# A whole masked last tile, the samples' state as the moving operand, and a head's squares in one row

## The chip, the cores and the metric

One core of one Trainium2 chip runs the whole program. The metric is the device time of one execution in microseconds, the median of the runs taken.

## What is computed

The reference is one inference step of a trunk of two layers with D = 1024. The input is a prompt of 2064 tokens (16 learned ones and 2048 more) and a group of 8 samples with one token each and a state from before. Each layer is `x <- LayerNorm(alpha*x + mixer(x))`. The mixer projects x to 10 x 512 channels and 8 gates, runs three groups of heads on them and projects the result back:

- A, a gated linear recurrence over time;
- B, retention: 4 heads of 128 channels; a score of key by query times a fixed decay, and a state S of 128 x 128 that decays and gains key by value;
- C, the gated delta rule: 4 heads of 128 channels; keys are normed, each token has a decay and a strength, and a chunk of 64 tokens needs the inverse of a triangular matrix of its keys' products; it too carries a state S of 128 x 128 per head.

```python
v_new = u - jnp.einsum('bhik,bhkv->bhiv', w, s)
att = jnp.einsum('bhid,bhjd->bhij', q, k) * decay
o = jnp.einsum('bhik,bhkv->bhiv', q * jnp.exp(gc)[..., None], s) + jnp.einsum('bhij,bhjv->bhiv', att, v_new)
s = s * jnp.exp(g_last)[..., None] + jnp.einsum('bhik,bhiv->bhkv', k * jnp.exp(g_last - gc)[..., None], v_new)
```

The samples take one such step each, from their own state, and everything is in float32. The outputs are the new activations and all new states.

## The kernel before

Each layer goes over its tokens in two halves (`sblock`): 1024 prompt tokens, then 1040 prompt tokens and the 8 samples. A half is a row of stages (`STAGES`): four K stages (the delta heads' keys), and then the heads of the groups A, B and C, one stage each. A stage projects its channels: 24 matmuls for each slab of 128 channels and each block of 512, 384 or 280 tokens (x and the weights are split in a high and a low float32r part, three products). Into these the head work of earlier stages is mixed: it is written as generators, and a `Pump` takes a step of them after so many projection matmuls. After both halves come the output projection with the LayerNorm, row tile by row tile, and into it the samples' work is mixed in the same way (`samples_delta`, `samples_ret`).

That order is not the final one. A `Recorder` notes every operation with a cost, simulates the engines and writes each engine's instructions in the order in which they came out (`order`): of the operations that are ready, the earliest noted goes first. All instructions are issued by this, so nearly all have line 273 in the profile, and they are told apart by their tiles. The order on each engine is then fixed. TensorE's, VectorE's, ScalarE's, GpSimd's and SP's queues each run in that order; hardware semaphores hold back what isn't ready.

The names that the change touches:

- `tl` in `sblock` lists a half's groups: two of 4 tiles with 128 tokens, and in the second half one more tile of 16 tokens, the tail. Its third entry, `R`, is the tile's height, and all work on the tail is cut to `R`: tiles of 16 rows, 16 columns, or both.
- `gates_c` makes the gates of all tokens as columns (`gtok`, `gg`, `bt`), `valid` masks the empty rows of the ninth tile.
- `keys_bg` makes for each delta head the decay matrix (`pdt`: two float32r matmuls and a bfloat16 one) and the squares of its keys in chunks of 64 (`pk`: 128 rows, 64 columns of weights, 64 moving columns; two chunks side by side in the array's column halves). There is one PSUM tile `pk` for a group of 4 tiles, and a generator step behind each.
- `inverses` and `solve` invert the triangular matrices; the tail's has 16 rows.
- `delta_bg` runs a delta head: `prep` (transposes `ptk`, `ptv`, `ptq`, products with the inverse `pw` and `pu`, keys by queries `qk`), `chain` (from chunk to chunk: the state's product `pz`, its update `pd`), `outs` (`po`), `norm` (`pno`). For the tail, `chain` reads the state with two products, `pz<-stg,wt` and `pz<-stg,qT`.
- `retention_bg` runs a retention head with tiles of 128 tokens: `prep` (`qk`, `ptk`, `ptv`), `chain` (scores by values, the state's product, its update `pd`), and at the end a norm and `pno`. For the tail the products are `po<-tk`, `po<-str,qT` and `pd<-tk`.
- `samples_delta` and `samples_ret` load a head's 8 states of 128 x 128 (`sv`) and multiply each as weights with two columns (key and query) or one (query): `ps<-swork,sv` and `ps<-scol,sv`. Then `outer` forms the new states.

In float32 a matmul of the program is two MATMUL instructions in the profile, each with a weight load of its own; a transpose is one.

```python
for b in range(NS):
    PE.matmul(pb[:, 16 + 2 * b:18 + 2 * b], sv[:, 0, b], kq[:, h, b], start=True, stop=True)
```

Of the kernel before, what the change touches and what calls it, by code (L numbers as in the profile page):

```python
# [343 lines left out]
def hymba_step(ctx: ExitStack, tc: tile.TileContext, x0t, x0, win, wab, wout, wg, vec, fbc, const, rope,  # L344
# [31 lines left out]
    mean_l = C("ones128").to_broadcast([128, 128])  # L376
    identb = cst.tile([128, 128], BF, name="identb")
# [25 lines left out]
    def pz2():  # L403
        return [psum.tile([128, 512], F32, tag="pz", name="pz", bufs=2).rearrange("p (t c) -> p t c", t=4)
                for _ in range(2)]
# [150 lines left out]
    def layer(l):  # L556
# [43 lines left out]
        def sblock(sb):  # L600
# [71 lines left out]
            tl = [(0, 4, 128), (4, 4, 128)] + ([(8, 1, 16)] if samp else [])  # L672
# [34 lines left out]
            def gates_c():  # L707
# [3 lines left out]
                if samp:  # L711
                    G.memset(gtok[:, 8], 0.0)
                for t in range(NT):
                    n = min(128, ts - t * 128)
                    PE.transpose(pg[:n, t, :], gab[:16, t * 128:t * 128 + n], ident[:16, :16])
                for n, ta, tb in ((128, 0, 8), (24, 8, 9))[:1 + samp]:
                    V.tensor_copy(gtok[:n, ta:tb], pg[:n, ta:tb, 0:8])
                    V.tensor_tensor(gtok[:n, ta:tb], gtok[:n, ta:tb], pg[:n, ta:tb, 8:16], op=OP.add)
# [6 lines left out]
                if samp:  # L725
                    V.tensor_tensor(gg, gg, C("valid").unsqueeze(2).to_broadcast([128, 9, 4]), op=OP.mult)
# [3 lines left out]
                V.tensor_scalar(bt[:, :NT], bt[:, :NT], 0.5, 0.5, op0=OP.mult, op1=OP.add)  # L730

# [12 lines left out]
                if samp:  # L744
                    G.memset(ssk[:, 8], 0.0)
# [21 lines left out]
            def keys_bg(h, kT):  # L767
                dt = wk.tile([128, 9, 64], F32, tag="dt", name="dt", bufs=1)
                for t4, nt, R in tl:
                    m = min(64, R)  # L770
                    gm, gl = (wk.tile([128, 4, 64], F32R, tag="gm", name="gm", bufs=2) for _ in range(2))
                    for e, x in enumerate((gm, gl)):
                        V.tensor_tensor(x[:R, :nt, :m], C("maskc")[:R, :m].unsqueeze(1).to_broadcast([R, nt, m]),
                                        ggp[:R, e, t4:t4 + nt, h:h + 1].bitcast(F32).to_broadcast([R, nt, m]),
                                        op=OP.mult)
                    pd = pt("pdt")[:, :256].rearrange("p (t i) -> p t i", i=64)
                    for e, x in enumerate((gm, gl)):
                        PE.matmul(pd[:R, :nt, :m], m1r[:R, :R], x[:R, :nt, :m], start=(e == 0), stop=False)
                    PE.matmul(pd[:R, :nt, :m], identb[:R, :R],
                              negb[:R, :m].unsqueeze(1).to_broadcast([R, nt, m]), start=False, stop=True)  # L780
                    A.activation(dt[:R, t4:t4 + nt, :m], pd[:R, :nt, :m], AF.Exp)
# [921 lines left out]
    for l in range(DEPTH):  # L1703
        layer(l)
# [107 lines left out]
```

## Time and profile before

| | us |
|---|---|
| median of 3 runs | 3141.41 |
| lowest, highest | 3139.7, 3144.42 |
| the profiled execution | 3134.19 |
| its span, first to last instruction | 3132.2 |

The span holds 47396 instructions. In the profile an engine's busy time is the union of its instructions; matmuls are pipelined, and their ends are modelled, so the time from one matmul's start to the next tells more than its duration. PE is the matmul part of TensorE and PEld its weight loads, DVE is VectorE, ACT ScalarE, POOL GpSimd. The view in order of time merges neighbouring instructions of one form into a row: start, latency from the first start to the last end, engine, line, operation, output and inputs, shape of the array (rows*columns), the moving operand, and the count. Some matmul records can be missing from a trace, so a count may be low by one.

### The profile page before, as it was taken

The page shows a single profiled execution, that of the slowest core. Times are in us where ns is not written, and L with a number is a line of the kernel's source. Part 1 is how long each engine was busy: PE and PEld are TensorE (multiplying, and loading weights), DVE is VectorE, ACT ScalarE, POOL GpSimd, SP SyncE. Part 2 cuts the span into 40 slices and gives each one's busy share as a digit, 9 for nine tenths or more (in the row PEclk, how much of TensorE's full clock was granted, in tenths as well). Part 3 has the DMA queues.
Part 4 walks back from the last instruction along what each step waited for, and adds up shares of the span by engine and source line. Part 5 has one row for each costly group of instructions (what it writes and reads, how often), then busy time and mean ns, then how long its engine had stood idle before and what let it go on. Part 6 is the DMA issues. An engine that isn't in the chain of part 4 may idle for free. (4 is left out here: it accounts for less than half of the span.)

```text
span 3132.2 us, 47396 instructions
## 1 busy us (share of the span) xinstructions
PE 3089.2 (99%) x18876; PEld 2707.9 (86%) x18876; DVE 2038.0 (65%) x3736; ACT 1294.2 (41%) x2732; POOL 678.5 (22%) x651
## 2 busy tenths in 40 slices
PE   8999999999999999999999999999999999999999
PEld 6888888899999999788778888888999999997886
DVE  6976565679756565656469765655897565656564
ACT  4455444543454454311144544444434544543100
POOL 2222132222222231011022222222222222311110
PEclk9999999999999999999999999999999999999999
DMA  4121111321111113555231212112211111136641
GB/s 154 63 70 48 57 50 58 110 82 51 49 54 59 46 57 96 179 175 168 95 115 56 70 48 66 52 57 96 85 50 50 54 59 43 61 92 195 183 145 59
DMA packets 137060, 262.96 MB, mean 84 GB/s; under 512 B 24368, under 2 KB 79600, under 8 KB 136840
## 3 DMA queue, kind: packets, MB, share of 16 engines
q1 hardware_dynamic: 113640, 179.91, 18.5%
q0 software_dynamic: 23200, 80.04, 7.1%
q8 instruction: 148, 2.42, 0.3%
q14 instruction: 72, 0.59, 0.1%
HBM read 195.13 MB, written 65.04 MB: 83 GB/s over the span
## 5 line engine op out<-in xcount | busy, mean ns | idle before, releaser
L273 PE MATMUL pj<-arena 128*128 128x512 f32 (+3 forms) x9760 | 2114.1, 360 | 14.3 <-ACT arena L273 7.6
L273 PEld LDWEIGHTS pj<-arena 128*128 128x128 f32 (+1 forms) x9760 | 1625.5, 187 | 170.6 <-ACT arena L273 8.2
L273 POOL TENSOR_TENSOR arena<-raw,arena 128x1024 fp32r<-128x1024 f32 x159 | 399.5, 2512 | 1077.5 <-ACT arena L273 886.4
L273 ACT CAST arena<-raw 128x1024 fp32r<-128x1024 f32 x180 | 189.0, 1050 | 302.4 <-PE pj L273 163.9
L273 DVE SCALAR_TENSOR_TENSOR stg<-stg,eg,pd 128x128 f32<-128x128 f32 x264 | 90.8, 344 | 117.6 <-PE pd L273 116.4
L273 PE MATMUL pj<-arena,ah 128*128 128x512 f32 x512 | 166.0, 401 | 1.3 <-ACT arena L273 1.3
L273 ACT COPY ur<-pj 128x512 f32<-128x512 f32 (+2 forms) x160 | 80.4, 503 | 146.1 <-PE pj L273 146.0
L273 ACT ACT_TABLE_LOAD x106 | 136.0, 1283 | 4.5 <-DVE vT L273 1.9
L273 ACT COPY sw<-pj 64x512 f32<-64x512 f32 (+2 forms) x160 | 79.9, 500 | 103.2 <-PE pj L273 65.7
L273 PEld LDWEIGHTS pj<-arena,ah 128*128 128x128 f32 x512 | 96.7, 189 | 24.5 <-ACT arena L273 1.8
L273 PE MATMUL pj<-arena,al 128*128 128x512 f32 (+1 forms) x296 | 111.6, 398 | 0.1
L273 ACT ACTIVATE g<-pj 128x512 f32<-128x512 f32 (+2 forms) x120 | 61.8, 515 | 109.9 <-PE pj L273 108.9
L273 PE MATMUL pd<-kv 128*128 128x128 f32 x512 | 99.9, 277 | 3.5 <-DVE kv L273 2.6
L273 PEld LDWEIGHTS pz<-stg,wq 128*128 128x128 f32 x512 | 89.7, 189 | 12.5 <-DVE stg L273 2.7
L273 PE MATMUL pz<-stg,wq 128*128 128x128 f32 x512 | 99.6, 276 | 0.8 <-DVE stg L273 0.4
L273 PEld LDWEIGHTS pd<-kv 128*128 128x128 f32 x512 | 86.8, 190 | 13.7 <-issue 2.8
L273 DVE SCALAR_TENSOR_TENSOR g<-g,pj 128x512 f32<-128x512 f32 (+2 forms) x120 | 69.5, 579 | 39.5 <-ACT g L273 38.5
L273 ACT ACTIVATE wq<-pz,eg 64x128 f32<-64x128 f32 x128 | 44.1, 361 | 122.9 <-DVE kv L273 55.1
L273 PE MATMUL po<-arena,ah 128*128 128x512 f32 x288 | 93.9, 400 | 0.0
L273 ACT CAST bh<-mb 128x512 fp32r<-128x512 f32 x32 | 19.6, 620 | 171.3 <-PE po L273 107.9
L273 DVE SCALAR_TENSOR_TENSOR qT<-ur,gcw,qT 128x1024 f32<-128x1024 f32 (+1 forms) x48 | 75.0, 1562 | 18.4 <-ACT qT L273 18.3
L273 DVE SCALAR_TENSOR_TENSOR kT<-ur,gcw,kT 128x1024 f32<-128x1024 f32 (+1 forms) x48 | 74.0, 1541 | 19.2 <-ACT kT L273 18.7
(388 smaller groups left out, 5057.7 us busy)
## 6 DMA issues: line engine op xcount, KB each, us to landing
raw<-in_win SPq DMA_DIRECT2D x160, 512.0 KB, 3.3
ma<-mix_d SPq DMA_DIRECT2D x31, 512.0 KB, 5.1
mix_d<-g POOLq DMA_DIRECT2D x24, 520.0 KB, 3.3
mix_d<-g POOLq DMA_DIRECT2D x24, 512.0 KB, 3.4
raw<-in_wout SPq DMA_DIRECT2D x24, 512.0 KB, 4.4
xr<-in_x SPq DMA_DIRECT2D x16, 512.0 KB, 5.1
x_d<-yo POOLq DMA_DIRECT2D x16, 512.0 KB, 3.3
sv<-row_d POOLq DMA_DIRECT2D x16, 512.0 KB, 4.7
```

Of the source, the lines that this page charges most:

```text
L273: return lambda *args, **kw: self._r.note(self._n, op, lambda: f(*args, **kw), args, kw)
```

## The change

- The tail becomes a whole tile: the last 128 tokens of the prompt's second half (columns `np_ - 128` to `np_`), of which only the last 16 count. Masks and zeros (`cl`, loaded once by four small DMAs after two clears) keep the other 112 out: gates and strengths are multiplied by `tmask`, retention's key and score decays come from `tkdec` and `tdec`, and the delta head's inverse lies in the last 16 columns of a cleared tile. All tail matmuls have 128 rows and 128 columns then; the two reads of the state in the delta head's chain become one. The delta tail borrows group 0's `wq` and attention tile and the tile `ttbd` of the inverses. Its decay matrix is made in 128 x 64, and one DMA stores or loads all of a head's decay matrices where there were two.
- The squares of a head's keys are written one behind the other, without a step between, all 16 into one PSUM bank; the tail's two squares go to a second bank.
- The samples' products take the state as the moving operand (`from_state`): eight products with 32 columns of weights, of which one or two count, in the array's four column strips, 128 moving columns each; ScalarE copies the 128 x 256 result, and two transposes bring it back to columns.

The diff, cut to its core (elsewhere it replaces `:R` by whole tiles in the same way):

```diff
--- before.py
+++ after.py
...
+    cl = cst.tile([128, 13], F32, name="cl")
+    tmask, tkdec, tdec, teps = cl[:, 0:1], cl[:, 1:5], cl[:, 5:9], cl[:, 9:13]
+    def tail_constants():
+        G.memset(cl[:, 0:9], 0.0)
+        G.memset(teps, EPS)
+        a = _C["dret"][0] + 127
+        for dst, src in ((tmask, const[0:16, _C["ones"][0]:_C["ones"][1]]),
+                         (tkdec, const[0:16, _C["kdect"][0]:_C["kdect"][1]]),
+                         (tdec, const[0:16, a:a + 385:128]),
+                         (teps, const[0:16, _C["epsr"][0]:_C["epsr"][1]])):
+            SP.dma_start(dst[112:128], src)
...
-            tl = [(0, 4, 128), (4, 4, 128)] + ([(8, 1, 16)] if samp else [])
...
+                    c0 = min(t * 128, np_ - 128)
+                    PE.transpose(pg[:, t, :], gab[:16, c0:c0 + 128], ident[:16, :16])
...
+                    V.tensor_tensor(gg[:, 8], gg[:, 8], tmask.to_broadcast([128, 4]), op=OP.mult)
...
+                    V.tensor_tensor(bt[:, 8], bt[:, 8], tmask.to_broadcast([128, 4]), op=OP.mult)
...
-                for t4, nt, R in tl:
-                    m = min(64, R)
-                    pk = pt("pk")[:, :256].rearrange("p (t i) -> p t i", i=64)
+                pks = [pt("pk").rearrange("p (t i) -> p t i", i=64) for _ in range(1 + samp)]
+                pks = [pks[0][:, 0:4], pks[0][:, 4:8], pks[-1][:, 0:1]]
+                for (t4, nt, c0), pk in zip(tl, pks):
                     for i in range(nt):
-                        for o in range(0, R, 64):
-                            c0 = (t4 + i) * 128 + o
-                            PE.matmul(pk[o:o + m, i, :m], kT[:, c0:c0 + m], kT[:, c0:c0 + m],
-                                      start=True, stop=True)
-                    if R == 128:
+                        for o in (0, 64):
+                            cc = slice(c0 + i * 128 + o, c0 + i * 128 + o + 64)
+                            PE.matmul(pk[o:o + 64, i], kT[:, cc], kT[:, cc], start=True, stop=True)
+                for (t4, nt, c0), pk in zip(tl, pks):
+                    if nt == 4:
                         V.tensor_tensor(ap[:, t4:t4 + 4, h, :], pk, dt[:, t4:t4 + 4], op=OP.mult)
                     else:
-                        V.tensor_tensor(apt[:16, :, h], pk[:16, 0, :16], dt[:16, 8, :16], op=OP.mult)
+                        V.tensor_tensor(apt[:, :, h], pk[96:128, 0, 48:64], dt[96:128, 8, 48:64], op=OP.mult)
                     gm = wk.tile([128, 4, 64], F32, tag="gm", name="gm", bufs=2)
-                    V.tensor_tensor(gm[:R, :nt, :m], pk[:R, :nt, :m],
-                                    C("id64")[:R, :m].unsqueeze(1).to_broadcast([R, nt, m]), op=OP.mult)
-                    V.tensor_reduce(out=ssk[:R, t4:t4 + nt, h], in_=gm[:R, :nt, :m], axis=AX, op=OP.add)
-                    yield
-                G.dma_start(dt_d[h, :, :512], dt[:, :8].rearrange("p t i -> p (t i)"))
-                if samp:
-                    G.dma_start(dt_d[h, :16, 512:528], dt[:16, 8, :16])
+                    V.tensor_tensor(gm[:, :nt], pk, C("id64").unsqueeze(1).to_broadcast([128, nt, 64]), op=OP.mult)
+                    V.tensor_reduce(out=ssk[:, t4:t4 + nt, h], in_=gm[:, :nt], axis=AX, op=OP.add)
+                    yield
+                G.dma_start(dt_d[h, :, :64 * NT], dt[:, :NT].rearrange("p t i -> p (t i)"))
...
-                        q.wt, q.at = small("wt", [128, 16]), small("at", [16, 16])
+                        q.wq, q.at, q.cis = gs[0].wq, gs[0].at, (1,)
...
+                    else:
+                        A.copy(ttbd[96:128, 0, 112:128], apt[:, :, h])
+                        G.memset(ttbd[96:128, 0, 96:112], 0.0)
+                        G.tensor_copy(q.wq[:, 0, 2], qT[:, c0 + 64:c0 + 128])
...
-                        A.copy(q.wt, pw[:, 0, :R])
+                        A.copy(q.wq[:, 0, 3], pw[:, 0, 64:128])
+                        G.tensor_copy(kk[64:128, 0], kk[64:128, 1])
+                        G.memset(kk[0:64, 0], 0.0)
...
-                        for ci, (o, n) in enumerate(((0, 64), (64, 64)) if q.R == 128 else ((0, 16),)):
+                        for ci in q.cis:
                             pz = q.pz[i // 2][:, i % 2, ci]
-                            if q.R == 128:
-                                PE.matmul(pz, q.wq[:, i, 2 * ci:2 * ci + 2].rearrange("p e c -> p (e c)"), S,
-                                          start=True, stop=True)
-                            else:
-                                PE.matmul(pz[:16], q.wt, S, start=True, stop=True)
-                                PE.matmul(q.pz[0][:16, 0, 1], qT[:, q.c0:q.c0 + 16], S, start=True, stop=True)
-                            if q.R == 128:
-                                V.tensor_tensor(uv[o:, 1, i], uv[o:, 0, i], pz[o:], op=OP.add)
-                            else:
-                                V.tensor_tensor(uv[:n, 1, i], uv[:n, 0, i], pz[:n], op=OP.add)
+                            PE.matmul(pz, q.wq[:, i, 2 * ci:2 * ci + 2].rearrange("p e c -> p (e c)"), S,
+                                      start=True, stop=True)
+                            o = 64 * ci if nt == 4 else 0
+                            V.tensor_tensor(uv[o:, 1, i], uv[o:, 0, i], pz[o:], op=OP.add)
                             yield
                             ps = p1("pd")
-                            if q.R == 128:
-                                PE.matmul(ps[:, :128], kk[:, 1 - ci, i], uv[:, 1, i], start=True, stop=True)
-                            else:
-                                PE.matmul(ps[:, :128], kk[:n, 1, i], uv[:n, 1, i], start=True, stop=True)
+                            PE.matmul(ps[:, :128], kk[:, 1 - ci, i], uv[:, 1, i], start=True, stop=True)
...
+            def from_state(pb, sv, cols, c0, n):
+                pr = pt("psv").rearrange("p (s c) -> p s c", s=4)
+                for b in range(NS):
+                    j = 32 * (b % 4)
+                    PE.matmul(pr[j:j + 32, b // 4], cols[:, c0 + n * b:c0 + n * b + 32], sv[:, 0, b], start=True, stop=True)
+                rw = wk.tile([128, 2, 128], F32, tag="gm", name="rw", bufs=2)
+                A.copy(rw, pr[:, 0:2])
+                for s in range(2):
+                    PE.transpose(pb[:, 128 + 128 * s:256 + 128 * s], rw[:, s], ident)
+                return pb[:, 128:384].rearrange("p (b e) -> p b e", e=32)
...
-                    for b in range(NS):
-                        PE.matmul(pb[:, 16 + 2 * b:18 + 2 * b], sv[:, 0, b], kq[:, h, b], start=True, stop=True)
-                    pv = pb[:, 16:32].rearrange("p (b e) -> p b e", e=2)
+                    pv = from_state(pb, sv, swork, 16 * h, 2)
...
-                    for b in range(NS):
-                        PE.matmul(pb[:, b:b + 1], sv[:, 0, b], qs[:, h, b:b + 1], start=True, stop=True)
-                    V.scalar_tensor_tensor(out=o[:, h], in0=pb[:, 0:8], scalar=GAM[h], in1=o[:, h],
+                    pv = from_state(pb, sv, scol.rearrange("p c e h b -> p (c e h b)"), 128 + 8 * h, 1)
+                    V.scalar_tensor_tensor(out=o[:, h], in0=pv[:, :, 0], scalar=GAM[h], in1=o[:, h],
...
+                    if q.last:
+                        V.scalar_tensor_tensor(out=sn[:, 0, 0], in0=pa[:, 0], scalar=tdec[:, h:h + 1],
+                                               in1=C("minc"), op0=OP.mult, op1=OP.mult)
...
-                    kd = C("kdec" if R == 128 else "kdect")[:R, h:h + 1]
-                    A.activation(kv[:R, 0, :nt], pk[:R, :nt], AF.Copy, scale=kd)
+                        PE.transpose(pk[:, i, :], kT[:, c0 + i * 128:c0 + i * 128 + 128], ident)
+                    kd = (tkdec if q.last else C("kdec"))[:, h:h + 1]
...
-                        cc = slice(c0 + i * 128, c0 + i * 128 + R)
-                        PE.matmul(po[:R, i], qT[:, cc], S, start=False, stop=True, skip_group_check=True)
+                        cc = slice(c0 + i * 128, c0 + i * 128 + 128)
+                        PE.matmul(po[:, i], qT[:, cc], S, start=False, stop=True, skip_group_check=True)
                         ps = p1("pd")
-                        PE.matmul(ps[:, :128], kv[:R, 0, i], kv[:R, 1, i], start=True, stop=True)
-                        V.scalar_tensor_tensor(out=S, in0=S, scalar=GAM[h] ** R, in1=ps[:, :128],
+                        PE.matmul(ps[:, :128], kv[:, 0, i], kv[:, 1, i], start=True, stop=True)
+                        V.scalar_tensor_tensor(out=S, in0=S, scalar=GAM[h] ** (16 if q.last else 128), in1=ps[:, :128],
                                                op0=OP.mult, op1=OP.add)
```

## Rows read from the trace of the kernel before

**Rows 1.** The page: busy time of the engines, granted clock by slice, a copy's group.

```profile
PE 3089.2 (99%) x18876; PEld 2707.9 (86%) x18876; DVE 2038.0 (65%) x3736; ACT 1294.2 (41%) x2732; POOL 678.5 (22%) x651
...
PEclk9999999999999999999999999999999999999999
...
L273 ACT COPY ur<-pj 128x512 f32<-128x512 f32 (+2 forms) x160 | 80.4, 503 | 146.1 <-PE pj L273 146.0
```

**Rows 2.** Waits of TensorE: line waited for, us in total, times, longest.

```profile
PE ps L273 <- DMA sv<-in_sret: 4.3, 1, 4.3
```

**Rows 3.** TensorE in order of time: start us, latency us, instructions; projection alone, a last transpose.

```profile
98.84 13.54 PE L273 MATMUL pj<-arena 128*128 128x512 f32 x59
...
920.66 1.55 PE L273 MATMUL pj<-arena 128*128 128x384 f32 x8
922.14 0.23 PE L273 MATMUL pno<-ct,tk 16*128 16x16 f32 x1
922.30 1.14 PE L273 MATMUL pj<-arena 128*128 128x384 f32 x5
```

**Rows 4.** TensorE in order of time, layer 0: a retention head's last tiles.

```profile
1041.63 0.38 PE L273 MATMUL pz<-str,qT 128*128 128x128 f32 x2
...
1042.00 1.29 PE L273 MATMUL pj<-arena 128*128 128x384 f32 x6
1043.12 0.27 PE L273 MATMUL ptv<-ct,vT 128*16 128x128 f32 x1
1043.15 1.21 PE L273 MATMUL pj<-arena 128*128 128x384 f32 x6
...
1048.08 0.39 PE L273 MATMUL po<-tk 16*16 16x128 f32 x2
1048.40 1.17 PE L273 MATMUL pj<-arena 128*128 128x280 f32 x6
1049.50 0.39 PE L273 MATMUL po<-str,qT 128*16 128x128 f32 x2
...
1050.24 0.45 PE L273 MATMUL pj<-arena 128*128 128x384 f32 x1
```

**Rows 5.** TensorE in order of time, layer 0: delta heads' tails.

```profile
914.21 0.48 PE L273 MATMUL pd<-tk 16*128 16x128 f32 x2
...
914.93 1.30 PE L273 MATMUL pj<-arena 128*128 128x280 f32 x8
...
998.33 0.21 PE L273 MATMUL qk<-qT,kT 128*16 128x16 f32 x2
998.47 0.53 PE L273 MATMUL pj<-arena 128*128 128x280 f32 x2
...
1113.40 0.39 PE L273 MATMUL pz<-stg,wt 128*16 128x128 f32 x2
...
1113.94 0.40 PE L273 MATMUL pj<-arena 128*128 128x280 f32 x1
```

**Rows 6.** TensorE in order of time, layer 0: a head's squares.

```profile
60.13 0.57 PE L273 MATMUL pk<-kT 128*64 128x64 f32 x12
60.63 0.50 PE L273 MATMUL pj<-arena 128*128 128x512 f32 x1
61.06 0.69 PE L273 MATMUL pk<-kT 128*64 128x64 f32 x16
61.68 1.66 PE L273 MATMUL pj<-arena 128*128 128x512 f32 x6
```

**Rows 7.** TensorE in order of time, layer 0: a delta head's samples.

```profile
1323.29 1.93 PE L273 MATMUL ps<-swork,sv 128*128 128x2 f32 x16
1325.07 0.48 PE L273 MATMUL pj<-arena,ah 128*128 128x512 f32 x1
```

**Rows 8.** Busy time by stretch: PE, PEld, DVE, ACT, POOL, granted clock, DMA share, GB/s.

```profile
1275.00:1280.00 5.00, 1.71 (x5) 1.55 (x6) 1.44 (x4) 1.64 (x2) 0.00 (x0) 0.70 0.77 248
```

More of the change, by code (lines that the diff above doesn't have):

```diff
@@ L401, in pj, with pz2 @@
         return psum.tile([128, 512], F32, tag="pj", name="pj", bufs=2)
-    def pz2():
+    def pz2(n=2):
         return [psum.tile([128, 512], F32, tag="pz", name="pz", bufs=2).rearrange("p (t c) -> p t c", t=4)
-                for _ in range(2)]
+                for _ in range(n)]
     def p1(tag):
@@ L777, in keys_bg @@
                     for e, x in enumerate((gm, gl)):
[L778 to L781, printed above, removed]
+                        PE.matmul(pd[:, :nt], m1r, x[:, :nt], start=(e == 0), stop=False)
+                    PE.matmul(pd[:, :nt], identb, negb.unsqueeze(1).to_broadcast([128, nt, 64]), start=False, stop=True)
+                    A.activation(dt[:, t4:t4 + nt], pd[:, :nt], AF.Exp)
                     yield
@@ L875, in inverses @@
                     pn = pt("pn")
-                    PE.transpose(pn[:4, :16], nf[:16, 32:36], ident[:16, :16])
-                    A.copy(nbt, pn[:4, :16])
+                    PE.transpose(pn[:4, :128], nf[:, 32:36], ident)
+                    A.copy(nbt, pn[:4, 112:128])
                     a_ = a_[:, :16]
@@ L999, in prep @@
                     for i in range(nt):
-                        PE.matmul(pu[:R, i], inv_t(i), uv[:R, 0, i], start=True, stop=True)
-                    A.copy(uv[:R, 0, :nt], pu[:R, :nt])
+                        PE.matmul(pu[:, i], ttbd[:, i], uv[:, 0, i], start=True, stop=True)
+                    A.copy(uv[:, 0, :nt], pu[:, :nt])
                     yield
@@ L1079, in norm @@
                     for i in range(nt):
-                        PE.transpose(pn[:, i, :R], q.o[:R, i], C("swap") if R == 128 else ident[:R, :R])
-                    gv = g[:, c0:c0 + nt * R].rearrange("p (t c) -> p t c", t=nt)
-                    V.scalar_tensor_tensor(out=gv, in0=pn[:, :nt, :R], scalar=VV("nw"), in1=gv,
-                                           op0=OP.mult, op1=OP.mult)
+                        PE.transpose(pn[:, i], q.o[:, i], C("swap"))
+                    if nt == 4:
+                        gv = g[:, c0:c0 + 512].rearrange("p (t c) -> p t c", t=4)
+                    else:
+                        pn, gv = pn[:, 0, 112:128], g[:, np_ - 16:np_]
+                    V.scalar_tensor_tensor(out=gv, in0=pn, scalar=VV("nw"), in1=gv, op0=OP.mult, op1=OP.mult)
                     yield
-                gs = [alloc(i) for i in range(len(tl))]
+                gs = []
+                for i in range(len(tl)):
+                    gs.append(alloc(i))
                 yield from prep(gs[0])
```

171 lines of the change are left out of this document (78 added, 93 removed).

## The prediction

> **What bounds the kernel now.** The page comes first: TensorE is busy 99% of the span, VectorE 65%, ScalarE 41%, GpSimd 22%, and the granted clock is 0.9 or more in every slice [rows 1]. A busy TensorE is not yet a bound, so the waits come second: of all its waits on a transfer only one is long, 4.3 us in one place [rows 2], and the idle time in all is 3132.2 - 3089.2 = 43 us. So the time is the sum of the intervals between the starts of TensorE's matmuls, and I read those in the third view, TensorE's instructions in order of time. There the "us" of a row holds latency, so I use differences of starts only. One more word: in float32 a matmul shows as two instructions, here passes; a transpose shows as one.
>
> **The pace and the price of a visit.** Alone, a projection pass of 512 columns starts every (13.54 - 0.39)/58 = 0.227 us; one of 384 columns every (1.55 - 0.34)/7 = 0.173 us [rows 3]. Against that pace small work has a price, and the array's shape decides it.
> - Other shapes: eight passes stand ahead of the 16*128 transpose in 1.48 us where 8 x 0.173 = 1.38, 0.10 more; the five behind it show 1.14 - 0.34 = 0.80 for four intervals, 0.11 more [rows 3]. I take 0.20 for the way into another shape and back, beside a visit's own stretch.
> - Whole array (128*128): two products of two passes take 1041.63 to 1042.00 = 0.37 us, and the six projection passes behind them take 1.12 us where 6 x 0.173 = 1.04, so 0.08 is paid behind: 0.45 for four passes [rows 4]. Each further pass is 0.11, so two passes alone are 0.03 + 0.11 + 0.08 = 0.22. One transpose: 1043.12 to 1043.15, + 0.08 = 0.11.
>
> **Part 1, the tail.** All eight delta heads and eight retention heads (4 heads, 2 layers) of the second half have a tail of 16 tokens, whose matmuls are 16 wide or 16 high. The change makes it 128 x 128 with zeros in masks, so the visits go and whole-array prices take their place.
> - Retention, scores times values: 1048.08 to 1048.40 = 0.32, + 0.20 = 0.52 -> 0.22 [rows 4]. The delta head's two products with the inverse have the same form (two passes, 16 wide), priced alike: 3 x 0.30 x 8 = 7.2 us.
> - Retention, state read and update: 1049.50 to 1050.24 = 0.74, 0.94 in all -> 0.45: 0.49 x 8 = 3.9 us [rows 4].
> - Delta, update and output: 914.21 to 914.93 = 0.72, 0.92 -> 0.45: 8 x 0.47 = 3.8 us. The two state reads: 1113.40 to 1113.94 = 0.54, 0.74 -> 0.22, now one product: 8 x 0.52 = 4.2 us. Keys by queries, both kinds: 998.33 to 998.47 = 0.14, 0.34 -> 0.22: 16 x 0.12 = 1.9 us [rows 5].
> - Last transpose: 0.16 + 0.20 = 0.36 -> 0.11: 16 x 0.25 = 4.0 us [rows 3].
> The tail's other transposes have 128 moving columns on either side and stay at 0.11. Sum 25.0 us.
>
> **Part 2, the keys.** Now a head's two groups of squares stand as two visits. The one projection pass between takes 60.63 to 61.06 = 0.43 where 0.227 is its pace, 0.20. Twelve passes of squares take 60.13 to 60.63 = 0.50, sixteen 61.06 to 61.68 = 0.62 [rows 6]: 0.03 for a pass, and 0.14 for the ends of a visit. One row in one bank saves 0.20 + 0.14 = 0.34 a head, 16 heads: 5.4 us. The tail's square, priced as the keys by queries above, 0.34, becomes two squares in the row, four passes at 0.03 = 0.12: 1.8 us. The tail's decay matrix now takes three short 16*16 passes, most often in two visits, each priced as the keys by queries: 0.68. Whole, it is three passes of 64 columns with two float32r weight loads: no row has that form, so at least 0.22, as for two passes, at most 0.68, no gain; I take 0.34 (three passes at the whole array's price), the nearest form: 8 x 0.34 = 2.7 us (0 to 3.7). Sum 9.9 us.
>
> **Part 3, the samples' products with the state.** Now the state is the weights: 16 passes of one or two columns take 1323.29 to 1325.07 = 1.78, + 0.08 = 1.86 us a head [rows 7]. With the state moving, each of eight products is 128 rows by 32 columns of weights, 128 moving columns, two passes, in four column strips. No row shows that form. The nearest are the squares: a pass of theirs takes 0.03, while 64 columns at the whole array's 0.11 for 128 would be 0.055, so two strips run at once [rows 6]. Four strips at once are then four times 0.11 = 0.44, + 0.14 + 0.20; behind ScalarE's copy come two transposes, 0.03 + 0.11 + 0.08: 1.00 us, a gain of 0.86, 16 heads: 13.8 us. Two at once: 1.44, a gain of 0.42, 6.7 us. One at a time, sixteen times 0.11 and the same rest: 2.32 us, a loss of 0.46, 7.4 us. I take four: the squares run as many strips at once as they have. With 43 us of idle time in the whole span, little of the gain can be hidden.
> The Trainium skill, page TensorE: Matmul & The Clock Gate, section Part 3, says that weight loads overlap matmuls in flight only where the row groups differ. All strips here share their rows; by that rule the one-at-a-time value would hold, and the whole sum would be 27.5 us. The squares, which share theirs too, speak against it.
>
> **What lies beside.** VectorE gets a mask for the gates, one more addition for the retention head's tail, two tail multiplies for one; ScalarE 16 copies of 128 x 256 and wider tail copies; GpSimd loses five clears in a stage and gains two copies and two clears a tail. All cost nothing while TensorE is 99% busy and these stand at 65%, 41% and 22% [rows 1]; without that cover the 16 copies alone, at no more than the 0.50 us of a 128 x 512 copy, would take up to 8 us [rows 1]. Transfers: one decay transfer for two per head on SP's and on GpSimd's queue, with 64 columns in place of 16; at the start four small ones on SP ahead of layer 0's own, which wait for GpSimd's clears: I put 0, at most 1 us, behind the first input loads. New waits: the tail borrows group 0's output buffer, its attention tile and the inverse tile, so its preparation stands behind group 0's output, where the order had put it already. In the samples' part TensorE waits for ScalarE's copy, and both tiles of the shared bank pair are held meanwhile; queued behind are the other sampler's product and the next layer's transposes, and projection passes fill in if the order written out by the cost model fits.
>
> **Sum.** 25.0 + 9.9 + 13.8 = 48.7 us. The profiled execution took 3134.19 us (span 3132.2), so 3085.5; the median of the runs shown is 7.2 us above it, and the same difference there gives 3141.4 - 48.7, 3093 us. A measurement here tells about 0.2%, 6 us, from no change.
>
> **Rivals.**
> 1. Strips don't run side by side. For: no row has the form. Against: the squares. One at a time: 34.9 - 7.4 = 27.5 us, 3114; two: 41.6 us, 3100.
> 2. The row of squares is broken: a pass of the decay matrix, noted earlier, becomes ready while they run and goes between, so the visits stay two. For: the order puts the earliest noted first among what is ready. Against: it has three steps' time before the squares. Gain 48.7 - 5.4 = 43.3 us, 3098.
> 3. Slower: the wait for ScalarE's copy between products and transposes. The order is fixed by a cost model; if the copy comes late, TensorE stands, as it did for 4.3 us on the state's load [rows 2], in a stretch with 1.71 us busy of 5 and a granted clock of 0.70, a mix of full and half [rows 8]. It decides from 48.7/16 = 3.0 us a head on. At 3.7 us (a wait of 2, and as much again at half clock) the sum is 59.2 - 48.7 = 10.5 us more, 3152. Against: ScalarE is 41% busy, and no other wait of TensorE is like it.
> 4. The gain is met by chance in the order: all engines' instructions are put in a new order by the cost model, and the 43 us of idle time and the low clock stretches come out otherwise. Worth 10 us either way, without a sign.
>
> **How the numbers follow.** Forecast 0.65, rival 1 0.17 (0.10 of it one at a time), rival 2 0.10, rival 3 0.04, a gain of under 6 us, which takes rival 1's worst and twice rival 4's size together, 0.04. Faster in the first three, 0.92; same 0.04; slower 0.04. The range reaches from the forecast less 16 (rival 4's 10, the decay matrix's and the edges' 6) to rival 1's 3114 and 3 more: 3077 to 3117.
>
> **What would show it.** In TensorE's order of time: tail rows of 128*128 whose stretch is 0.14 us or 0.37 us, projection passes ahead of them at pace; one row of 32 (36 in the second half) passes of squares per head; 16 state passes in about 0.6 us, then two transposes. VectorE's and ScalarE's busy time should hardly move, TensorE's busy time should fall by the gain, and its idle time stay near 43 us. State passes in 1 us or more make rival 1 true; idle time before the transposes rival 3; a busy TensorE that falls by less than 27 us would show that the prices by visit are wrong.

## The result and the profile after

The kernel after takes 3102.45 us (median of 4 runs, 3097.41 to 3105.11) beside 3142.63 us for the kernel before: the ratio is 0.9881 (95% interval 0.9859 to 0.9904), 40.2 us. In a second measurement, with other runs of both, it was 3101.43 beside 3131.59 us: 0.9899 (0.9884 to 0.9914), 30.2 us. The forecast was 3093 in 3077 to 3117, faster at 0.92. Sign and range held; of the 48.7 us worked out part by part 30 to 40 came, by the measures below some 30.

The page of the kernel after, the lines that answer to [rows 1]:

```profile
PE 3050.6 (98%) x18908; PEld 2693.4 (87%) x18908; DVE 2049.8 (66%) x3758; ACT 1297.2 (42%) x2740; POOL 695.0 (22%) x649
...
PEclk9999999999999999999999999999999999999999
```

The span is 3098.7 us. TensorE is busy 38.6 us less than before; its idle time (span less busy) is 48.1 us where it was 43.0. The other engines moved little. So the time came out of TensorE's own work, less than forecast, and a little went back into waiting.

**The tail**, TensorE in order of time in the kernel after, answering to [rows 3 to 5]: first start, us, instructions. A row's form is that of its first instruction; neighbouring projection passes of other lengths share the row.

```profile
1041.66 0.38 PE L273 MATMUL po<-tk 128*128 128x128 f32 x2
1041.80 1.16 PE L273 MATMUL pj<-arena 128*128 128x280 f32 x6
1042.80 0.38 PE L273 MATMUL po<-str,qT 128*128 128x128 f32 x2
1043.02 0.39 PE L273 MATMUL pd<-tk 128*128 128x128 f32 x2
1043.16 7.03 PE L273 MATMUL pj<-arena 128*128 128x384 f32 x39
...
1054.54 0.27 PE L273 MATMUL pno<-ct,tk 128*128 128x128 f32 x1
1054.56 1.63 PE L273 MATMUL pj<-arena 128*128 128x280 f32 x9
...
2437.76 0.38 PE L273 MATMUL pw<-ttbd,tk 128*128 128x128 f32 x2
2437.90 0.60 PE L273 MATMUL pj<-arena 128*128 128x384 f32 x2
...
2461.09 0.38 PE L273 MATMUL pd<-tk 128*128 128x128 f32 x2
2461.31 0.39 PE L273 MATMUL po<-tk,attb 128*128 128x128 f32 x2
2461.46 1.79 PE L273 MATMUL pj<-arena 128*128 128x280 f32 x12
```

Two passes take 0.14 us from start to start, four 0.36 or 0.37, the last transpose 0.02: the whole-array prices that the forecast took from the full tiles hold for the tail.

**The squares**, the same view, answering to [rows 6]: a head of the first half, then one of the second half.

```profile
57.48 1.15 PE L273 MATMUL pk<-kT 128*64 128x64 f32 x32
58.56 0.73 PE L273 MATMUL pj<-arena 128*128 128x512 f32 x2
...
2233.11 0.33 PE L273 MATMUL pk<-kT 128*64 128x64 f32 x2
2233.37 0.30 PE L273 MATMUL pdt<-gm,m1r 128*128 128x64 f32 x1
2233.59 0.45 PE L273 MATMUL pk<-kT 128*64 128x64 f32 x8
2233.98 0.30 PE L273 MATMUL pdt<-gm,m1r 128*128 128x64 f32 x1
2234.11 0.21 PE L273 MATMUL pdt<-negb,identb 128*128 128x64 bf16 x1
2234.25 0.91 PE L273 MATMUL pk<-kT 128*64 128x64 f32 x22
2235.09 0.44 PE L273 MATMUL pj<-arena 128*128 128x384 f32 x1
2235.47 0.34 PE L273 MATMUL pk<-kT 128*64 128x64 f32 x4
2235.73 1.49 PE L273 MATMUL pj<-arena 128*128 128x384 f32 x7
```

In the first half 32 passes stand together and take 1.08 us. In the second half the tail's decay matrix goes between: this head has four visits to the squares, not one, and six of the eight heads there are split. Over all heads the trace has 30 visits, where the kernel before had 41 and the forecast wanted 16.

**The samples**, the same view, answering to [rows 7]:

```profile
1374.18 0.28 PE L273 MATMUL ps<-swork,ct 128*128 128x8 f32 x2
1374.39 0.64 PE L273 MATMUL psv<-sv,swork 128*32 128x128 f32 x16
1374.96 0.73 PE L273 MATMUL po<-arena,ah 128*128 128x512 f32 x2
...
1376.01 0.38 PE L273 MATMUL ps<-ct,rw 128*128 128x128 f32 x2
1376.14 0.48 PE L273 MATMUL po<-arena,ah 128*128 128x512 f32 x1
```

Sixteen passes in 0.57 us, for 1.78 before: four strips run at once. Projection passes fill the time of ScalarE's copy, and the two transposes take 0.13.

**The waits of TensorE** in the kernel after, answering to [rows 2]: us in total, times, longest.

```profile
PE qk L273 <- ACT kv L273: 5.1, 3, 2.4
...
PE psv L273 <- DMA sv<-in_sret: 3.1, 1, 3.1
```

The wait for the state's load is 3.1 us for 4.3 (in the second execution below it is 6.2 us in two places). The first row is new in its size: in the kernel before this wait is 1.0 us in one place.

**Two ways of counting** are needed below. First, each run is listed with its mean granted clock, between 0.992 and 0.998. Time x clock, roughly what the run would take at full clock, is nearly the same for all runs of a kernel: 48 runs of the kernel before, taken beside the experiments, lie between 3125.9 and 3143.7 us, but their products between 3118.8 and 3124.8, not far from what three decimals of a clock can resolve (0.0005 is 1.6 us). The median product is 3120.7 to 3121.9 in each of the four measurements that these runs come from. Second, in a profiled execution the granted clock is either full or half. As the clock's loss I count half of TensorE's busy time inside the stretches at half, an estimate: 8.8 us before, 8.3 us after. Taken off TensorE's busy time this leaves 3080.4 us before and 3042.3 after, 38.1 us less. Half clock while TensorE stands costs no work and isn't counted here. Time x clock does count it (4.1 us in the execution before, 1.6 in the one after), so it shows 2.5 us less of gain there.

| kernel | median us | ratio to before (95%) | time x clock | busy | idle | lost to clock while busy | visits to squares |
|---|---|---|---|---|---|---|---|
| before | 3131.6 to 3142.6 | | 3121 | 3089.2 | 43.0 | 8.8 | 41 |
| after | 3102.45 | 0.9881 (0.9859, 0.9904) | 3091.6 | 3050.6 | 48.1 | 8.3 | 30 |
| after, again | 3101.43 | 0.9899 (0.9884, 0.9914) | 3089.5 | 3053.7 | 49.6 | 11.4 | 30 |
| samples only | 3116.60 | 0.9941 (0.9925, 0.9956) | 3109.6 | 3073.0 | 41.4 | 2.6 | 41 |
| tail only | 3113.17 | 0.9928 (0.9911, 0.9944) | 3101.8 | 3066.1 | 45.8 | 8.2 | 37 |
| tail and squares | 3114.96 | 0.9938 (0.9921, 0.9956) | 3102.9 | 3060.7 | 47.2 | 5.0 | 30 |
| one row | 3098.57 | 0.9882 (0.9864, 0.9901) | 3086.1 | 3047.8 | 49.1 | 8.3 | 17 |
| strip twice | 3098.70 | 0.9896 (0.9879, 0.9913) | 3089.8 | 3046.6 | 48.7 | 3.3 | 30 |
| before, other order | 3133.23 | 0.9997 (0.9986, 1.0008) | 3122.0 | 3089.5 | 46.5 | 9.3 | 38 |
| after, other order | 3104.53 | 0.9907 (0.9891, 0.9923) | 3088.6 | 3054.8 | 49.1 | 15.1 | 26 |
| one row, other order | 3105.01 | 0.9910 (0.9894, 0.9925) | 3089.5 | 3054.3 | 53.4 | 18.2 | 17 |
| one row, longer load | 3095.90 | 0.9876 (0.9858, 0.9895) | 3083.5 | 3046.2 | 45.6 | 6.4 | 17 |
| ... and kv's place | 3104.80 | 0.9914 (0.9900, 0.9929) | 3087.3 | 3052.2 | 51.6 | 18.6 | 17 |
| ... or two steps later | 3112.40 | 0.9937 (0.9922, 0.9953) | 3094.6 | 3052.6 | 58.8 | 16.3 | 17 |

Median and ratio are of the timed runs, time x clock is their median; busy, idle and lost are of the profiled execution.

### The profile page after: what moved, and what is told of

Its sections match the earlier page's. It is cut to its first block, busy times and chain, and to the rows that moved or that the text cites. A ratio compares the mean times of both kernels' runs of the same rounds, so it can differ in the third digit from the quotient of the medians.

```text
span 3098.7 us, 47484 instructions
## 1 busy us (share of the span) xinstructions
PE 3050.6 (98%) x18908; PEld 2693.4 (87%) x18908; DVE 2049.8 (66%) x3758; ACT 1297.2 (42%) x2740; POOL 695.0 (22%) x649
## 5 line engine op out<-in xcount | busy, mean ns | idle before, releaser
L273 DVE SCALAR_TENSOR_TENSOR vT<-ur,gcw,vT 128x1024 f32<-128x1024 f32 (+1 forms) x48 | 78.0, 1624 | 10.5 <-ACT vT L273 10.0
L273 DVE TENSOR_TENSOR kv<-kv,pz 128x128 f32<-128x128 f32 (+1 forms) x128 | 37.0, 289 | 71.5 <-PE pz L273 70.8
L273 PE MATMUL qk<-qT,kT 128*128 128x128 f32 x544 | 77.5, 278 | 5.2 <-ACT kv L273 5.1
```

Of the source, the lines that this page charges most:

```text
L273: return lambda *args, **kw: self._r.note(self._n, op, lambda: f(*args, **kw), args, kw)
```

## The experiments

**The change taken apart.** Three kernels.

Samples only: the kernel before, with the two places that multiply by the state changed.

```diff
-for b in range(NS):
-    PE.matmul(pb[:, 16 + 2 * b:18 + 2 * b], sv[:, 0, b], kq[:, h, b], start=True, stop=True)
-pv = pb[:, 16:32].rearrange("p (b e) -> p b e", e=2)
+pv = from_state(pb, sv, swork, 16 * h, 2)
...
```

> The kernel before with the samples' products alone changed. Four strips at once, as the profile after shows them: 0.57 us for 16 passes and 1.0 us a head in all against 1.86, so 13.8 us faster than the kernel before, 3128 us. Two strips at once would give 6.7 us, one at a time 7.4 us slower. Rival, the order by chance: TensorE's busy time falls by 13 to 14 us all the same, but its idle time moves by several us, so the time comes out up to 10 us to either side of 3128.

Time x clock 11.5 us under the kernel before (3109.6 beside 3121), by medians 20.2: the clock was 0.998 in four of its six runs, where the kernel before had 0.994 to 0.997, and some 8 us of its gain are that. The busy time without the clock's loss fell by 10.0 us, the idle time by 1.6. Four strips it is, with 10 to 12 us for the 13.8. Its median lies 11 us below 3128, just outside what I had allowed for chance.

Tail only: the kernel after, with the samples' products as before, and a bank and a step for each group of squares.

```diff
-pks = [pt("pk").rearrange("p (t i) -> p t i", i=64) for _ in range(1 + samp)]
-pks = [pks[0][:, 0:4], pks[0][:, 4:8], pks[-1][:, 0:1]]
-for (t4, nt, c0), pk in zip(tl, pks):
+for t4, nt, c0 in tl:
+    pk = pt("pk")[:, :64 * nt].rearrange("p (t i) -> p t i", i=64)
...
```

> The masked whole tail alone: samples' products as before, and each group's squares in a bank of its own with a step between, as before. The tail's term 25.0 us, the whole decay matrix 0 to 3.7 us, and of the tail's square little, since it stays a visit: 25 to 28 us faster than before, 3114 to 3117 us. Against the tail with one row of squares it has 37 visits to the squares for 30, so it should be 7 x 0.34 = 2.4 us slower than that. If prices by visit were wrong, TensorE's busy time would fall by less than 20 us.

19 us by time x clock, short of 25 to 28; busy without the clock's loss fell by 22.5, idle time rose by 2.8. So the prices by visit are right in kind and too high in size.

Tail and squares: the kernel after, with the samples' products as before.

> The kernel after with the samples' products put back. By the prediction's terms 25.0 + 9.9 = 34.9 us faster than before. Theory: the row of squares is broken, 30 visits in this kernel's order where the prediction had 16 or 17, 13 to 14 too many at 0.34 us, so 30 us faster, 3112 us. If it gains less than 27 us, the rest went into idle time and half clock, which then stand in its profile above the kernel before's. If parts add up, its gain and the samples' gain together make the change's 40 us.

18 us by time x clock: nothing more than the tail alone, though seven visits are gone. Busy without the clock's loss is 2.2 us less than in the tail alone (7 x 0.34 = 2.4 was expected), idle time 1.4 more, and the rest lies within the scatter. It gained less than 27 us, and for that case the expectation named idle time and half clock. Idle time is above the kernel before's, by 4.2 us; half clock isn't, with 5.0 us lost for 8.8. The larger part is the tail's work, which fell by less than its prices. The parts do add up: 18 and 11.5 make 29.5, and the whole change has 29 to 32 by the same measure.

**One row.** The tail's two squares become one whole-array product, noted first, so a head's 32 squares need one bank and wait for one.

```diff
+if samp:
+    pkt = pt("pkt")[:, :128]
+    PE.matmul(pkt, kT[:, np_ - 128:np_], kT[:, np_ - 128:np_], start=True, stop=True)
+pk = pt("pk").rearrange("p (t i) -> p t i", i=64)
 for i in range(8):
     for o in (0, 64):
...
-V.tensor_tensor(gm[:, :nt], pk, C("id64").unsqueeze(1).to_broadcast([128, nt, 64]), op=OP.mult)
+V.tensor_tensor(gd, pkt, ident, op=OP.mult)
```

> The kernel after, with the tail's squares taken by one whole-array product of 128 columns ahead of the others, so that a head's squares need one bank and wait for one. In the order that results the squares stand in 17 visits, not 30. Theory (broken row): 13 x 0.34 = 4.4 us off, eight whole-array products of 0.22 us on (1.8), sixteen passes of 0.03 to 0.05 off (0.5 to 0.8): 3 to 3.5 us faster than the kernel after. Rival, the order by chance: TensorE's busy time falls by that, and idle time moves by as much or more, so the time comes out anywhere from 7 us slower to 13 us faster than the kernel after.

Time x clock is 3.4 to 5.5 us under the two measurements of the kernel after, and busy time without the clock's loss 2.9 us under the first: the broken row was worth about what the visits say. By medians the two kernels can't be told apart, and this one has a stall of 5.2 us where the kernel after has one of 2.4 (below). In order of time, a head of the second half now shows (from the kernel with the longer load, below, which has the same change):

```profile
2229.37 0.46 PE L273 MATMUL pkt<-kT 128*128 128x128 f32 x2
...
2231.07 1.15 PE L273 MATMUL pk<-kT 128*64 128x64 f32 x32
```

**The kernel after again.**

> The kernel after itself, beside the experiments of the same call. Theory: the runs of one kernel differ by their mean granted clock, so time x clock is nearly constant, 3092 us, and lies 29 to 30 us under the kernel before's 3121; the rest of the gain by medians is clock. Rival: the work itself gained 40 us, and time x clock is 38 to 40 us lower. If time x clock is constant within 3 us for each kernel, the clock is what scatters the runs.

Its five products run from 3084.6 to 3092.7, a median of 3089.5 beside 3121.9 for the kernel before: 32 us. The theory holds against its rival, but the products of one kernel are constant within 8 us here, not 3. So the 40 us of the first comparison are about 30 of the kernel and the rest clock: the four runs of the kernel before there, 3139.7 to 3144.4, lie at the top of its range, where its later runs have a clock of 0.994 or 0.995.

**One strip twice.** The order of the eight products of a head.

```diff
-for b in range(NS):
+for b in (0, 4, 1, 5, 2, 6, 3, 7):
     j = 32 * (b % 4)
```

> The kernel after, the samples' eight products issued in the order 0, 4, 1, 5, 2, 6, 3, 7, so that two products for the same strip of the array follow each other. If TensorE starts passes strictly in the order of issue, a pass behind one of its own strip holds all others: 0.45 to 0.66 us more a head, 7 to 11 us slower than the kernel after, and the 16 passes take about 1.1 us for 0.57. If each strip takes its passes for itself, no change: 16 passes in 0.57 us and a time within 3 us of the kernel after at the same clock.

3089.8 beside 3089.5 at the same clock, and the 16 passes stay at the same length; from this kernel's order of time:

```profile
1365.19 0.67 PE L273 MATMUL psv<-sv,scol 128*32 128x128 f32 x16
```

(0.64 or 0.65 in the kernel after.) Starts still come in four groups of four. So in this order, too, four strips run at once, and it cost no more than 0.02 us a head. In which order a group's passes stood in the queue, the trace doesn't tell; so whether each strip takes its passes for itself stays open.

**Another order of the same work.** One constant of the cost model by which the order is made, in the kernels before, after, and with one row.

```diff
-SLACK = {"PE": 0.2, "DVE": 0.07, "ACT": 0.07, "POOL": 0.1, "SP": 0.05}
+SLACK = {"PE": 0.25, "DVE": 0.07, "ACT": 0.07, "POOL": 0.1, "SP": 0.05}
```

> The kernel before with the same constant of the order's cost model changed (0.25 for 0.20). It prices the chance of the order without the change: theory, time x clock moves by up to 6 us either way from 3121 (its order has 38 visits to the squares for 41, 1 us less), and the clock by 0.001 or 0.002, so the time comes out between 3122 and 3142 us. If a kernel's order were worth no more than 2 us, the differences of idle time between the kernels of this study would have to be their own.

> The kernel after with one constant of the order's cost model changed (the time that a result of another engine is taken to need before TensorE may use it, 0.25 for 0.20), so that the same work stands in another order. Theory of chance in the order: time x clock moves by up to 6 us either way, the waits of more than 1 us stand in other places, and the stall of 2.4 us at the second delta head's tail moves or goes. If the stalls are the change's own, they stay where they are and time x clock stays within 2 us. Its order has 26 visits to the squares for 30: 1.4 us less.

> The kernel with the squares in one row (17 visits), with the same other constant. Theory: against the other kernel of that constant it has 9 visits fewer, so 2 to 4 us less; its stall of 5.2 us at 819 us, which comes of VectorE's step standing behind a GpSimd tensor_tensor of 2.4 us, moves with the order, and if it goes the time is 4 to 8 us under the one-row kernel's. If the stall belongs to the change, it stays.

The kernel before doesn't move: 0.9997, time x clock 1 us more. The kernel after moves by 1 to 3 us at the same clock, but its waits change place: the stall at 819 us is gone from its list, the delta heads' state reads wait for VectorE's state updates in nine places instead, 12.3 us, and 15.1 us are lost to the clock where it was 8.3 and 11.4. With one row the expected gain of visits doesn't come in the time (3089.5 beside 3088.6, nine visits fewer). It does come in the busy time without the clock's loss, 3.6 us where 9 x 0.34 = 3.1; but idle time is 4.3 us more, the stall stays (5.9 us), and 18.2 us are lost to the clock. So an order is worth 1 to 4 us of work, and by the mean clock of the timed runs 3 to 4 us more (0.9950 for 0.9962, and 0.9948 for 0.9958 with one row), and it can eat a gain of three.

**The waits themselves.** First where the new stall of the kernel after comes from, VectorE, GpSimd and TensorE in order of time around it:

```profile
811.13 3.06 DVE L273 SCALAR_TENSOR_TENSOR s<-y,s 128x1048 f32<-128x1048 f32 x1
...
817.88 2.38 DVE L273 TENSOR_TENSOR_SCAN s<-r,hcar,ix 128x1040 f32<-128x1040 f32 x1
...
820.85 0.68 DVE L273 TENSOR_TENSOR sn<-qk,ct 128x512 f32<-128x512 f32 x1
...
810.67 2.41 POOL L273 TENSOR_TENSOR arena<-raw,arena 128x1024 fp32r<-128x1024 f32 x1
...
821.36 0.71 PE L273 MATMUL qk<-qT,kT 128*128 128x128 f32 x4 [2.39 <-ACT kv L273]
```

and the same steps in the kernel before:

```profile
813.70 1.23 DVE L273 SCALAR_TENSOR_TENSOR s<-y,s 128x1048 f32<-128x1048 f32 x1
...
815.91 2.62 POOL L273 TENSOR_TENSOR arena<-raw,arena 128x1024 fp32r<-128x1024 f32 x1 [2.76 <-ACT arena L273]
```

The same VectorE step takes 1.23 us alone and 3.06 when GpSimd's subtraction of two tensors started 0.46 us ahead of it: it ends 1.1 us after GpSimd does (814.19 and 813.08), as if it had waited for it. In the one-row kernel the step takes 3.36 us, and the stall is 5.2. Behind the step stands the scan, and for the scan ScalarE's copy waits, and TensorE for the copy. But the lost 1.83 us can't be the whole cause: the scan ends at 820.26 here and 2 us later, at 822.23, in the kernel before, which has no such stall. What differs is how far TensorE is. In the kernel after:

```profile
809.14 1.05 PE L273 MATMUL qk<-qT,kT 128*128 128x128 f32 x8
...
810.38 8.59 PE L273 MATMUL pj<-arena 128*128 128x384 f32 x48
```

and in the kernel before:

```profile
819.85 2.38 DVE L273 TENSOR_TENSOR_SCAN s<-r,hcar,ix 128x1040 f32<-128x1040 f32 x1
...
817.64 1.05 PE L273 MATMUL qk<-qT,kT 128*128 128x128 f32 x8
...
819.93 4.43 PE L273 MATMUL pj<-arena 128*128 128x384 f32 x24
824.20 0.38 PE L273 MATMUL qk<-qT,kT 128*128 128x128 f32 x2
```

The kernel after begins the head 8.5 us earlier and is through with its projection passes at 818.97, ahead of the scan; the kernel before still has passes up to 824.20. Nor need it be this one step. In the one-row kernel in the other order it has no GpSimd step beside it, and the stall is 5.9 us:

```profile
817.20 1.23 DVE L273 SCALAR_TENSOR_TENSOR s<-y,s 128x1048 f32<-128x1048 f32 x1
...
825.59 1.23 PE L273 MATMUL qk<-qT,kT 128*128 128x128 f32 x4 [5.93 <-ACT kv L273]
```

There two smaller steps ahead of it are held up beside GpSimd (2.02 and 2.14 us), as one is in the kernel before (2.04). So the stall is one of the order, TensorE's against VectorE's; how much of it is VectorE's time beside GpSimd, no run separates.

Then the load of the state. The cost model is told that transfers issued by GpSimd take longer:

```diff
-end = max(dma, start + 1.6) + 0.3
+end = max(dma, start + 1.6) + 0.3 + (op.nbytes / 1.5e5 if e == "POOL" else 0.0)
```

> The one-row kernel, with the cost model told that a transfer issued by GpSimd takes longer by its bytes (3.5 us more for the 512 KB of a sample's state; the trace shows 4.5 to 7.7 us from issue to landing), so that other work is put between a state's load and the products that read it. Theory: the waits of TensorE for the state, 3 to 6 us, go, and with them 3.4 us at half clock behind the one at 1264 us; order up to there is the one-row kernel's, so its stall of 5.2 us at 819 us stays. 3 to 8 us under the one-row kernel: time x clock 3080 to 3084. Rival: what is put between moves other work, new waits of the same size stand elsewhere, and the time stays within 3 us.

The waits for the state are gone from the list, and time x clock, 3083.5, lies in the range expected. But that is 2.6 us under the one-row kernel, just short of the 3 to 8, and a change of that size the rival allows as well. Busy time by stretch (PE, PEld, DVE, ACT, POOL, granted clock, DMA share, GB/s), the kernel after and then this one:

```profile
816.00:832.00 16.00, 13.54 (x90) 12.71 (x89) 11.81 (x26) 4.07 (x7) 1.14 (x2) 0.89 0.09 35
1262.00:1272.00 10.00, 6.87 (x35) 4.42 (x35) 6.32 (x9) 4.65 (x8) 1.67 (x1) 0.83 0.84 262
2168.00:2184.00 16.00, 16.00 (x88) 14.67 (x86) 14.08 (x46) 6.01 (x14) 2.33 (x3) 0.79 0.26 99
```

```profile
1262.00:1272.00 10.00, 9.75 (x44) 7.56 (x43) 7.46 (x12) 7.47 (x10) 1.93 (x1) 1.00 0.83 268
```

From 1262 to 1272, with TensorE busy 9.75 of 10 us for 6.87, the granted clock stays at full for 0.83. This kernel, 3095.90 us, is the fastest of the study: 6 to 8 us under the kernel after at the same clock (runs from 3082.9 to 3084.3, against 3084.6 to 3092.7 in nine of the other).

Last, the stall at 819 us, tried in two ways on that kernel: two tiles exchange places, so that ScalarE's copy needn't wait for the scan; or each retention head's preparation is put two steps later.

```diff
-kv, sn = big(("a1", "a3")[gi], "kv", bufs=1), big(("a2", "a4")[gi], "sn", bufs=1)
+kv, sn = big(("a4", "a3")[gi], "kv", bufs=1), big(("a2", "a1")[gi], "sn", bufs=1)
```

> The last one-row kernel (with the longer load time in the cost model), with two tiles of the retention heads in each other's places: group 0's scaled keys stand where the recurrence's y stood, and group 1's scores where its r stood. In the stall of 5.2 us at 819 us, ScalarE's copy of those keys waits for VectorE's scan, whose r held the place; y is done 7 us earlier. Theory: that stall goes, with the half clock behind it (4 us lost), 5 to 9 us under the kernel before this one: time x clock 3076 to 3080, 3088 us. Rival: the step behind it, the scores' multiplication, stands behind the same scan on VectorE, so TensorE waits there in its place, and the time stays within 3 us.

```diff
+for _ in range(2):
+    yield
 yield from prep(gs[0])
```

> The last one-row kernel (with the longer load time), with each retention head's preparation two steps later, behind more projection passes. Theory: the scan is done before the preparation needs it, the stall of 5.2 us goes, 4 to 8 us less. Rival, the order by chance: every head's order changes, stalls of 1 to 5 us stand in other places, and time x clock moves by up to 6 us either way from 3083.

Both missed. TensorE in order of time with the longer load, then with the exchanged places:

```profile
813.41 4.61 PE L273 MATMUL pj<-arena 128*128 128x384 f32 x25
823.21 1.22 PE L273 MATMUL qk<-qT,kT 128*128 128x128 f32 x4 [5.19 <-ACT kv L273]
```

```profile
819.30 1.13 PE L273 MATMUL pj<-arena 128*128 128x384 f32 x5
825.64 1.97 PE L273 MATMUL ptv<-ct,vT 128*128 128x128 f32 x8 [5.21 <-DVE sn L273]
```

The wait for the copy is gone, and a wait of the same length for the scores' multiplication, which stands behind the scan on VectorE, takes its place, as the rival had it. The work was 3.8 us worse at the same clock, a little more than the rival allowed, with new waits of 2 to 3 us. The two steps cost 11 us, with idle time up by 13. VectorE's own lateness there was not mended by any run, so what the stall is worth stays open.

## Why the prediction was right, and where its sum was wrong

The result lies in the range and on the forecast's side, and the mechanism was right: TensorE bounds the kernel, and what is taken off its work comes off the time. The sum was 48.7 us; the busy time, without what the clock took, fell by 38.1, and idle time rose by 5.1.

- **Part 1, with the decay matrix: 27.7 us forecast, 22.5 measured** (tail only). What was mis-sized is the price of a visit. "I take 0.20 for the way into another shape and back" came from one visit. Over the 146 visits of the kernel before that have a projection pass ahead and two behind, the pass ahead takes 0.084 us over its pace and the first one behind 0.101, 0.18 together; and 928 whole-array stretches pay 0.022 and 0.075, 0.10 for my 0.08, with the way in left at nothing. So a visit made whole saves 0.09 around it, not 0.12: over the 96 visits of this part about 3 us. The other 2 are in the stretches themselves, of which 13 us went, by the starts of all instructions, where my rows gave 15.
- **Part 2, squares: 7.2 us forecast, 2.2 measured** in busy time, none in the time. Rival 2 is what happened, in the second halves, and its counter-argument ("it has three steps' time before the squares") was the step that failed. The order isn't held by steps. The tail's decay matrix comes late, since VectorE's masks for it do (in the head shown, the last at 2233.06, when the row begins at 2233.11), and it was noted earlier, so it goes in between. It also takes its PSUM tile from the same ring of two as the squares, so the tail's squares wait until ScalarE has read it (2234.49) and stand apart. The price was right: 21 visits fewer were wanted, 7 came, 7 x 0.34 = 2.4; and the one-row kernel, 13 fewer still, gave 2.9 in busy time and 3.4 to 5.5 in time x clock for an expected 3 to 3.5.
- **Part 3, samples: 13.8 us forecast, 13.4 measured** (the busy time of the kernel after against tail and squares; alone it was 10.0, and 11.5 by time x clock). Four strips at once was right and so was each row's price: 0.57 us for 0.58, transposes 0.13 for 0.14. Rival 1 fell. The rule of the Trainium skill's page TensorE: Matmul & The Clock Gate, section Part 3, by which weight loads overlap matmuls in flight only where the row groups differ, doesn't describe these rows: all strips share their 128 rows, and starts of four come within 0.02 to 0.04 us.
- **What lies beside: nothing forecast, 5.1 us of idle time measured.** That TensorE's "idle time stay near 43 us" was wrong, and rival 4, chance in the order, worked against the change: TensorE came to a retention head's products ahead of VectorE's scan (5.1 us of waits for ScalarE's copy behind it, for 1.0 before). Rival 3 didn't happen: no wait for the copy of the samples stands in the list (under the other order one, of 1.4 us). Its "no other wait of TensorE is like it" passed over 6.8 us at the start of the program, which the change doesn't touch.
- **The base.** I added 7.2 us, by which the runs shown lay above the profiled execution. That was clock, not kernel: the later runs of the kernel before have medians of 3131.6 to 3136.8. Against the profiled execution alone the sum would have given 3085.5; the kernel after took 3100.5, 15 us more, which is the 10.6 us that the parts fell short, the 5.1 of idle time, less 0.5 of clock.

So a sum of 48.7 for 30 to 33 us ended only 9 us under the measured median. That is luck in part: the base it was taken from held about 10 us of low clock that the runs of the kernel after had less of.

## What to carry to other kernels

Price a visit to another array shape from many visits, and price what replaces it the same way: the saving is the difference of two small prices, and one row can be off by a third of it. Where instructions must stand together, look at what buffers they wait for, not at how many steps lie between; a ring of two shared with an earlier stage splits the row. Compare kernels at the same granted clock (time x clock) before you explain a difference of less than half a per cent; but look at the new waits too, for here most waits of 2 us brought half clock behind them. And before you blame a late step for a stall, look at where both engines stand in the kernel without the stall.

## What the runs showed of the hardware

- The scatter of the runs of one program, 3126 to 3144 us, is nearly all granted clock: the products with it lie within 6 us.
- A VectorE step on two tensors in SBUF stands while GpSimd works on two. In the 14 profiled executions the recurrence's step `s<-y,s` takes 1.21 to 1.25 us in the 144 places where no GpSimd step on two tensors runs beside it. In the 71 where one had started ahead of it, it takes 1.75 to 3.42 us and ends 1.08 to 1.11 us after that one's end. The Trainium skill's page SBUF — State Buffer, section SBUF: two separate sides, calls the port pair of the two an exclusive lock, held for a whole instruction; the rows agree.
- Where TensorE stood for 2 us or more, the granted clock was mostly at its lower level (1.2 of 2.4 GHz) soon after: 47 of 54 such waits in the 14 executions have a stretch at half clock that begins in the wait or within 4 us behind it, as behind the 2.39 us stall (0.89 in the 16 us from 816 in the kernel after). Five more stretches follow waits of 1.6 to 2.0 us. But for the stretch in which each execution ends, the other 14 all follow one piece of work in which TensorE counts as busy: sixteen passes of 16 rows and 8 columns. From 2168 on, with 16.00 of 16 us busy, the clock is 0.79 in the same kernel (both rows stand above), and this is what runs there:

```profile
2172.83 2.24 PE L273 MATMUL gs<-gab,ct 16*128 16x8 f32 x16
2175.00 7.25 PE L273 MATMUL pj<-arena 128*128 128x384 f32 x24
```

  Fourteen of the 28 places with these passes are followed by such a stretch, so it isn't them alone.
